# The lower query part of the prompt attention scores on all 128 rows

## The chip, the cores and the metric

The kernel runs on one core of a Trainium2 chip. The metric is device time in microseconds of one execution; before the change the median of three runs is 2746.48 us (2745.57 to 2746.51). Besides, one execution was recorded by the hardware profiler. PE is the matrix engine TensorE (PEld its weight loads, which can run under a product), DVE is VectorE, ACT is ScalarE, POOL is GpSimd, and SP issues most transfers.

## The reference

One layer of a hybrid decoder on a prompt of 1024 tokens and eight samples of eight tokens: a combined projection, then three branches (a gated linear recurrence, differential attention, cross-attention into 256 memory tokens), gates, an output projection and a feed-forward part with a convolution. All of it is float32. What the change touches is the prompt's differential attention, 8 heads with two components of 64 each:

```python
s = jnp.einsum('bqhcd,bkhcd->bhcqk', qi, k).astype(jnp.float32) * scale
s = jnp.where(kpos[None, :] <= qpos[:, None], s, NEG_INF)
p = jax.nn.softmax(s, axis=-1)
a = p[:, :, 0] - lam * p[:, :, 1]
return jnp.einsum('bhqk,bkhe->bqhe', a.astype(v.dtype), v)
```

So per head and component the scores are a product of 64-long queries and keys, for 1024 by 1024 tokens under a causal mask.

## The kernel before

Products run in a reduced float32 format (F32R). To keep precision an operand is split into an upper part (its copy in that format) and a lower part (what is left), and a product is the sum of upper times upper, upper times lower and lower times upper. The helper `mm3` (lines 162 to 165) issues those three as matmuls into one bank of PSUM; nearly all dense work goes through it.

Scores use a shorter way, since a component has only 64 features and the array has 128 rows. For component c, `qq[c]` holds the upper part of the queries in both halves of the partitions, and `kk[c]` holds the upper part of the keys in the half of its own and the lower part in the other. One product on all 128 rows (line 907) gives upper times upper and upper times lower at once. The lower part of the queries, `ql`, is one tile for both components: component 0 in partitions 0 to 63, component 1 in 64 to 127. The second product (line 909) reads only the half of its component, 64 rows of `ql` and 64 rows of `kk[c]`, and adds lower times upper into the same bank.

`attn(h)` works through the 1024 queries of a head in eight blocks of 128 (`qt`). Block `qt` needs 128 (qt + 1) keys, in chunks of at most 512 columns (at least 256 are computed), so 12 chunks per head and component, 24 pairs of products per head and 192 in all. DVE adds the mask (line 924), takes maxima (926); ACT takes exponentials (932); DVE normalizes and subtracts the second component (935 to 940). Later steps transpose the result (883) and multiply with the values.

The stage loops over eight heads. A unit projects the queries of a head (`unit(("q", h), ...)`), for three groups of tokens (384, 384 and 320 columns, 24 products each); `evac_q` takes each group out of PSUM: ACT copies the upper part of the half of its own, DVE subtracts for the lower part, POOL copies the upper part into the other half. Keys go likewise through `evac_k`. `attn(h)` is a generator in a lane of side work; `pump` advances it by rates while the next units' dense products are emitted, so that score steps lie between dense products. The tile layer places instructions on the engines' queues, derives the waits and hands out buffers; each engine then runs its queue in order.

Weights come as a stream: `Stream.ahead` loads a raw tile (`wr`, SP queue), ACT makes the upper part (`wh`, line 207) and POOL the lower (`wl`, line 209), one unit ahead, called after the first group of a unit. All these tiles, and `qq`, `ql`, `kk`, `e`, `ath`, `vh`, `pg`, share one pool of 42 buffers of 1088 columns (`slot`, `NSLOT`); eight banks of PSUM serve all products (`bank`).

Of the kernel before, what the change touches and what calls it, by code (L numbers as in the profile page):

```python
# [12 lines left out]
ALU = mybir.AluOpType  # L13
# [50 lines left out]
def layer_step(ctx: ExitStack, tc: tile.TileContext, a: dict, outs: list):  # L64
# [34 lines left out]
    def f(x):  # L99
        return x.bitcast(F32)  # L100
# [1 line left out]
    (o_yp, o_ys, o_kp, o_vp, o_mk, o_mv, o_lhp, o_lcp, o_fcp,  # L102
     o_ks, o_vs, o_lhs, o_lcs, o_fcs) = outs

# [1 line left out]
    later_q = deque()  # L106

    def later(fn, delay=1):
# [35 lines left out]
            for i in which:  # L144
                advance(lanes[i])

# [1 line left out]
    last_mm = [None]  # L148

    def load(dst, src):  # L150
        # a load is queued no earlier than the products that are being emitted
        ins = sp.dma_start(dst, src)
        if last_mm[0] is not None:
            tc.add_manual_dep(ins.ins, last_mm[0].ins.name,
                              mybir.DependencyInfo(mybir.DependencyClass.NoSync, mybir.DependencyReason.SCHED_ONLY),
                              reason="queue order")
# [7 lines left out]
        pe.matmul(ps, lhsT=lh, rhs=rl, start=False, stop=False)  # L164
        last_mm[0] = pe.matmul(ps, lhsT=ll, rhs=rh, start=False, stop=stop)  # L165

# [1 line left out]
    ident = const([128, 128], name="ident")  # L168
    pool.memset(ident, 0.0)
    pool.affine_select(out=ident, in_=ident, compare_op=ALU.not_equal, fill=1.0, base=0,  # L170
# [7 lines left out]
    pool.affine_select(out=causal, in_=causal, compare_op=ALU.is_ge, fill=NEG, base=0,  # L178
                       pattern=[[-1, 128]], channel_multiplier=1)

# [1 line left out]
    def cols(w, c0, width=128, k0=0, kn=8):  # L182
        return (w[k0 * 128:(k0 + kn) * 128, c0:c0 + width].rearrange("(k p) m -> p k m", p=128),
                [128, kn, width])
# [87 lines left out]
            for m2 in range(4):  # L272
                add(("d", g, p, m2), cols(w_down, m2 * 256, 256, g * NFG, NFG))

# [1 line left out]
    rawrow = slot([128, 6, 128], name="rawrow")  # L276
    rows = [rawrow[:, 0, :], rawrow[:, 1, :]]
    PV = {}
# [98 lines left out]
    def setup():  # L377
        put_params(1)
        ps = bank()
        pe.transpose(ps[:, 0:128], in_=frow[:, 0, :], identity=ident)  # L380
        pe.transpose(ps[:, 128:192], in_=frow[0:64, 1, :], identity=ident[:64, :64])
        act.copy(pf, ps[:, 0:192])
        ps = bank([128, NC, 32])
        for c in range(NC):
            pe.transpose(ps[:, c, :], in_=strow[:, c * 128:(c + 1) * 128], identity=ident[:32, :32])
        act.copy(stT, ps)
        yield False
        # lambda
        lprod = slot([128, 2, 64], name="lprod")
        dve.tensor_tensor(lprod[:, 0, :], lrow[:, 0, :], lrow[:, 1, :], ALU.mult)  # L390
        dve.tensor_tensor(lprod[:, 1, :], lrow[:, 2, :], lrow[:, 3, :], ALU.mult)
        dve.tensor_reduce(out=lam[:, 0:2], in_=lprod, axis=AX, op=ALU.add)
        act.activation(out=lam[:, 2:4], in_=lam[:, 0:2], func=AF.Exp)
        dve.tensor_tensor(lam[:, 4:5], lam[:, 3:4], lam[:, 2:3], ALU.subtract)
        dve.tensor_scalar(out=lam[:, 5:6], in0=lam[:, 4:5], scalar1=-LAM_INIT, scalar2=None, op0=ALU.add)
        dve.tensor_scalar(out=gsub, in0=P("g_subln"), scalar1=1.0 - LAM_INIT, scalar2=None, op0=ALU.mult)

        # softplus(-lambda), times 4 and -8
        spl = slot([128, 6, 8], name="spl")
        lo_ = PV["lru_lambda"][1]  # L400
        lm = pv[1][:, lo_:lo_ + 8]
        dve.tensor_scalar(out=spl[:, 0], in0=lm, scalar1=-1.0, scalar2=None, op0=ALU.mult)
        dve.tensor_tensor(spl[:, 1], lm, spl[:, 0], ALU.min)
        act.activation(out=spl[:, 2], in_=spl[:, 1], func=AF.Exp)
        dve.tensor_scalar(out=spl[:, 3], in0=spl[:, 2], scalar1=2.0, scalar2=None, op0=ALU.add)
        dve.reciprocal(out=spl[:, 3], in_=spl[:, 3])
        dve.tensor_tensor(spl[:, 3], spl[:, 2], spl[:, 3], ALU.mult)
        dve.tensor_tensor(spl[:, 4], spl[:, 3], spl[:, 3], ALU.mult)
        dve.memset(spl[:, 5], 1.0 / 17)
        for k in (15, 13, 11, 9, 7, 5, 3, 1):  # L410
            dve.tensor_tensor(spl[:, 5], spl[:, 5], spl[:, 4], ALU.mult)
            dve.tensor_scalar(out=spl[:, 5], in0=spl[:, 5], scalar1=1.0 / k, scalar2=None, op0=ALU.add)
        dve.scalar_tensor_tensor(out=spl[:, 5], in0=spl[:, 5], scalar=2.0, in1=spl[:, 3], op0=ALU.mult, op1=ALU.mult)
        dve.tensor_scalar(out=spl[:, 0], in0=spl[:, 0], scalar1=0.0, scalar2=None, op0=ALU.max)
        dve.tensor_tensor(spl[:, 0], spl[:, 0], spl[:, 5], ALU.add)
        for i, m in enumerate((4.0, -8.0)):
            dve.tensor_scalar(out=sp4[:, i, :], in0=spl[:, 0], scalar1=m, scalar2=None, op0=ALU.mult)
        yield False

    put_params(0)  # L420

    # memory tokens
    mss = tiny(2)
    mr = [tok_rstd(memtok[t], 128, mss[:, t:t + 1]) for t in range(2)]
    W.split(0)
# [14 lines left out]
                                 in1=mrb[:, 0:256], op0=ALU.mult, op1=ALU.mult)  # L440
        split(tf[:, 0:256], memh[c // 4][:, c % 4, :], meml[c // 4][:, c % 4, :])

    # x: three groups of tokens
    xs_d = [dpool.tile([128, T], F32, name=f"xsd{c}") for c in range(NC)]
    hh = [slot((128, T), F32R, "hh") for _ in range(NC)]
    hl = [slot((128, T), F32R, "hl") for _ in range(NC)]
# [24 lines left out]
            if c % 2 == 1:  # L471
                yield False

# [1 line left out]
    def dense(wh, wl, ah, al, g, nk=8, rate=()):  # L475
        g0, gn = GROUPS[g]
        ps = bank()
# [13 lines left out]
            pump(*[r / 2 for r in rate])  # L491

    def units(keys, evacs, ah, al, seq, rate=(1.0,), between=None):
        # several units at once, some groups of tokens for all of them before the others
        ws = [W.get(k) for k in keys]
        for n, gs in enumerate(seq):
            if n:
                between(n)
            for (wh, wl), evac in zip(ws, evacs):
                for g in gs:  # L500
                    ps = dense(lambda k: wh[:, k, :], lambda k: wl[:, k, :], ah, al, g)
                    evac(g, ps)
                    pump(*rate)
        W.ahead(1)

# [1 line left out]
    mk_d = [dpool.tile([128, 2, 256], F32, name=f"mkd{h}") for h in range(NMH)]  # L507
    mv_d = [dpool.tile([128, 2, 256], F32, name=f"mvd{h}") for h in range(NMH)]

    def mem_tail(p, kv):  # L510
        # keys of one head: feature on partitions
        ps = bank([128, 2, 256])
        for dc in range(2):
            for t in range(2):
                pe.transpose(ps[:, dc, t * 128:(t + 1) * 128], in_=kv[:, t, dc * 128:(dc + 1) * 128], identity=ident)
        kt = slot([128, 2, 256], name="mkt")
        act.copy(kt, ps)
        act.dma_start(mk_d[p], kt)
# [43 lines left out]
            e[1]()  # L562
        later_q.clear()

# [1 line left out]
    wrg = []  # L566
    for key in ("w_rg_a", "w_rg_i"):
        t = slot([128, NC, 128], name="wrg")
# [115 lines left out]
            load(pt_sb, a["page_table"].rearrange("b g -> (b g)").rearrange("(o n) -> o n", o=1))  # L684
    side.append(lru_out())

# [1 line left out]
    ms_d = [[dpool.tile([128, T], F32, name=f"msd{b}_{j}") for j in range(NC)] for b in range(2)]  # L688
    mh = [None] * NC
    ml = [None] * NC  # L690
# [60 lines left out]

    branch(0, load_lru, RB, spill_m(0), LAG0)

# [1 line left out]
    br_d = [[dpool.tile([128, T], F32, name=f"brd{b}_{h}") for h in range(NH)] for b in range(2)]  # L755
    done = [[0] * NH for _ in range(2)]
    kp_v = o_kp.rearrange("o b t h c d -> (o b t) (h c d)")
# [65 lines left out]
                pump(*RV)  # L823

    def subln_sums(sq, n):
        # sums of squares over partitions: one column of tokens per 128
        ps = bank()
        nt = (n + 127) // 128
        for i in range(nt):
# [16 lines left out]
    def attn(h):  # L846
# [5 lines left out]
        for t in range(7 + AVL + BC):  # L852
# [44 lines left out]
            if t < 8:  # L897
# [2 lines left out]
                ch = [(j, min(512, L - j)) for j in range(0, L, 512)]  # L900
                pss = {}
                for c in range(2):
                    r0 = 64 * c
                    for j, w in ch:
                        wm = max(w, 256)
                        ps = bank()
                        pe.matmul(ps[:, 0:wm], lhsT=qq[c][:, qt * 128:(qt + 1) * 128], rhs=kk[c][:, j:j + wm],
                                  start=True, stop=False)
                        last_mm[0] = pe.matmul(ps[:, 0:wm], lhsT=ql[r0:r0 + 64, qt * 128:(qt + 1) * 128],
                                               rhs=kk[c][r0:r0 + 64, j:j + wm], start=False, stop=True)  # L910
                        pss[c, j] = ps
                mx = tiny(4)
                sm = tiny(4)
# [27 lines left out]
                                         op0=ALU.mult, op1=ALU.add)  # L941
                av[qt] = e1
            yield t >= YT
# [1 line left out]
    smask = const([128, 2, 64], name="smask")  # L945
    dsel = const([128, 128], name="dsel")

# [141 lines left out]
    sample_setup()  # L1089
    for hp in range(4):  # L1090
        for h in (2 * hp, 2 * hp + 1):
            # queries: both halves of the partitions hold the upper parts; keys: upper and lower parts
            qq = [slot([128, TP], F32R, "qq") for _ in range(2)]
            ql = slot([128, TP], F32R, "ql")
            HALF = (slice(0, 64), slice(64, 128))

            def evac_q(g, ps):
# [3 lines left out]
                for c in range(2):  # L1101
                    own, other = HALF[c], HALF[1 - c]
                    act.copy(qq[c][own, cs], ps[own, 0:n])
                    dve.tensor_tensor(ql[own, cs], ps[own, 0:n], f(qq[c][own, cs]), ALU.subtract)
                    pool.tensor_copy(qq[c][other, cs], qq[c][own, cs])
                if g == 2:
                    act.copy(QKS[:, 0, h, :], ps[:, n:n + TS])

# [39 lines left out]
            lanes[1].append(sattn(h))  # L1148


# [1 line left out]
    MQ = {}  # L1152
    MSQ = {}
    for i in range(2):
# [185 lines left out]

    branch(2, load_br(1), RH, final_m)

# [1 line left out]
    x2_d = [dpool.tile([128, T], F32, name=f"x2d{c}") for c in range(NC)]  # L1344
    ob = [slot(name="ob") for _ in range(NC)]
    ssq = {}
# [23 lines left out]
    HOLD = 6  # L1370

    def residual(src, g):
        # tiles of the residual stream, read two ahead
        g0, gn = GROUPS[g]
        ts_ = {}

# [66 lines left out]
    drain((0,))  # L1443
    side.append(post_mix(2))

# [1 line left out]
    sfc = a["state_ffn_conv"].rearrange("o b j d -> (o b j) d")  # L1447
    fcs_v = o_fcs.rearrange("o b j d -> (o b j) d")
    acc = [None] * NC
# [56 lines left out]
        yield False  # L1506

    def ffn_tail_cut(j, pads):
        # as ffn_tail, one group of tokens after the other
        g, i = divmod(j, NFG)  # L1510
        fo = FO[g]
        cs = [slot(name="cv") for _ in range(2)]
# [54 lines left out]
            sp.dma_start(dst, yo[i][0:n])  # L1567
        yield False

    # the norm's factor is one number per token once the tokens are on the partitions  # L1570
    xtl, ytl, sct, ptl = {}, {}, {}, {}

    def pieces(g):
# [155 lines left out]
```

## Time and profile before

| | before |
|---|---|
| median of three runs | 2746.48 us |
| profiled execution, span from first to last instruction | 2744.3 us |
| PE busy | 2674.3 us (97%) |
| weight loads busy | 2536.1 us (92%) |
| DVE, ACT, POOL busy | 1254.8, 992.1, 891.0 us |
| mean granted TensorE clock | 0.987 of full speed |
| prompt attention, 500 to 1120 us: PE, DVE | 611.58, 389.68 us of 620 |

No time of the profiled execution beside its span is given; the median of the runs lies 2.2 us above that span. Busy time is the sum of an engine's instructions where they overlap counted once. Matmuls are pipelined: the shown duration of a product is longer than the distance to the next one, so what a product takes of the engine is read from the starts of successive products. A weight load that runs under the product before it costs nothing visible; one that starts only where its own product starts stands in the way.

### The profile page before, as it was taken

The page shows a single profiled execution, that of the slowest core. Times are in us where ns is not written, and L with a number is a line of the kernel's source. Part 1 is how long each engine was busy: PE and PEld are TensorE (multiplying, and loading weights), DVE is VectorE, ACT ScalarE, POOL GpSimd, SP SyncE. Part 2 cuts the span into 40 slices and gives each one's busy share as a digit, 9 for nine tenths or more (in the row PEclk, how much of TensorE's full clock was granted, in tenths as well). Part 3 has the DMA queues.
Part 4 walks back from the last instruction along what each step waited for, and adds up shares of the span by engine and source line. Part 5 has one row for each costly group of instructions (what it writes and reads, how often), then busy time and mean ns, then how long its engine had stood idle before and what let it go on. Part 6 is the DMA issues. An engine that isn't in the chain of part 4 may idle for free. (4 is left out here: it accounts for less than half of the span.)

```text
span 2744.3 us, 42962 instructions
## 1 busy us (share of the span) xinstructions
PE 2674.3 (97%) x16884; PEld 2536.1 (92%) x16884; DVE 1254.8 (46%) x2442; ACT 992.1 (36%) x2071; POOL 891.0 (32%) x891
## 2 busy tenths in 40 slices
PE   8999999999999999999999999989999999999997
PEld 7999899987888888899979999989999999999996
DVE  6465510267676665633234213277143343434357
ACT  6566521245445454434430212343321222222232
POOL 4355422423232333221111121353333333334234
PEclk9999999999999999999999999989999999999998
DMA  8311022221221212234755434132212111111133
GB/s 300 114 39 39 24 72 74 69 63 52 65 66 60 64 57 79 69 111 133 228 193 185 152 95 142 51 106 79 56 32 64 31 41 54 41 47 48 39 109 115
DMA packets 293472, 237.32 MB, mean 86 GB/s; under 512 B 16912, under 2 KB 276793, under 8 KB 293269
## 3 DMA queue, kind: packets, MB, share of 16 engines
q1 hardware_dynamic: 286484, 225.91, 26.3%
q10 hardware_dynamic: 6784, 8.65, 0.9%
q8 instruction: 133, 2.18, 0.3%
q14 instruction: 71, 0.57, 0.1%
HBM read 182.11 MB, written 52.40 MB: 85 GB/s over the span
## 5 line engine op out<-in xcount | busy, mean ns | idle before, releaser
L209 POOL TENSOR_TENSOR wl<-wr,wh 128x1024 fp32r<-128x1024 f32 x192 | 472.5, 2465 | 746.1 <-ACT wh L207 499.7
L163 PE MATMUL ps<-hh,wh 128*128 128x384 f32 (+1 forms) x1536 | 515.9, 336 | 3.3 <-DVE y L1015 1.2
L165 PE MATMUL ps<-hh,wl 128*128 128x384 f32 (+1 forms) x1536 | 504.9, 329 | 4.2 <-POOL wl L209 4.2
L164 PE MATMUL ps<-hl,wh 128*128 128x384 f32 (+1 forms) x1536 | 504.7, 329 | 0.0
L163 PE MATMUL ps<-h2h,wh 128*128 128x384 f32 (+1 forms) x1152 | 376.8, 328 | 3.2 <-ACT h2h L159 3.2
L164 PE MATMUL ps<-h2l,wh 128*128 128x384 f32 (+1 forms) x1152 | 377.2, 327 | 1.0 <-DVE h2l L160 1.0
L165 PE MATMUL ps<-h2h,wl 128*128 128x384 f32 (+1 forms) x1152 | 376.8, 327 | 0.9 <-POOL wl L209 0.9
L163 PEld LDWEIGHTS ps<-hh,wh 128*128 128x128 f32 x1536 | 290.5, 189 | 18.2 <-issue 11.1
L207 ACT CAST wh<-wr 128x1024 fp32r<-128x1024 f32 x199 | 208.0, 1051 | 255.6 <-PE ps L164 74.5
L165 PEld LDWEIGHTS ps<-hh,wl 128*128 128x128 f32 x1536 | 290.2, 189 | 7.1 <-POOL wl L209 4.8
L164 PEld LDWEIGHTS ps<-hl,wh 128*128 128x128 f32 x1536 | 290.6, 189 | 1.2 <-issue 1.0
L163 PE MATMUL ps<-bh,wh 128*128 128x384 f32 (+1 forms) x768 | 251.3, 328 | 0.0
L164 PE MATMUL ps<-bl,wh 128*128 128x384 f32 (+1 forms) x768 | 251.0, 327 | 0.0
L165 PE MATMUL ps<-bh,wl 128*128 128x384 f32 (+1 forms) x768 | 249.8, 327 | 0.0
L163 PEld LDWEIGHTS ps<-h2h,wh 128*128 128x128 f32 x1152 | 217.1, 189 | 3.7 <-ACT h2h L159 3.6
L164 PEld LDWEIGHTS ps<-h2l,wh 128*128 128x128 f32 x1152 | 217.2, 189 | 1.6 <-DVE h2l L160 1.5
L165 PEld LDWEIGHTS ps<-h2h,wl 128*128 128x128 f32 x1152 | 217.0, 188 | 1.1 <-POOL wl L209 1.1
L598 DVE TENSOR_SCALAR cv<-up,pf 128x1024 f32<-128x1024 f32 (+2 forms) x52 | 58.4, 1125 | 346.3 <-ACT up L586 176.1
L586 ACT COPY up<-ps 128x384 f32<-128x384 f32 (+1 forms) x144 | 63.9, 445 | 366.0 <-PE ps L165 350.5
L165 PE MATMUL ps<-ffh,wl 128*128 128x384 f32 (+1 forms) x576 | 189.3, 333 | 1.2 <-POOL wl L209 1.2
L164 PE MATMUL ps<-ffl,wh 128*128 128x384 f32 (+1 forms) x576 | 190.3, 332 | 0.0
L163 PE MATMUL ps<-ffh,wh 128*128 128x384 f32 (+1 forms) x576 | 188.1, 335 | 2.2 <-DVE acc L1679 1.6
(345 smaller groups left out, 5115.6 us busy)
## 6 DMA issues: line engine op xcount, KB each, us to landing
wr<-in_w_in_dram SPq DMA_DIRECT2D x72, 512.0 KB
wr<-in_w_up_dram SPq DMA_DIRECT2D x48, 512.0 KB
wr<-in_w_down_dram SPq DMA_DIRECT2D x32, 512.0 KB
msd<-sig SPq DMA_DIRECT2D x16, 544.0 KB
brl<-brd SPq DMA_DIRECT2D x16, 544.0 KB
mi<-msd SPq DMA_DIRECT2D x16, 544.0 KB
wr<-in_w_mem_kv_dram SPq DMA_DIRECT2D x16, 512.0 KB
pg<-in_cache_k_dram SPq DMA_DIRECT2D x128, 64.0 KB
```

The lines of the kernel that those rows point to most:

```text
L163: pe.matmul(ps, lhsT=lh, rhs=rh, start=start, stop=False)
L164: pe.matmul(ps, lhsT=lh, rhs=rl, start=False, stop=False)
L165: last_mm[0] = pe.matmul(ps, lhsT=ll, rhs=rh, start=False, stop=stop)
L207: (dve.tensor_copy if i == 1 else act.copy)(hi, t)
L209: eng.tensor_tensor(lo, t, f(hi), ALU.subtract)
L586: act.copy(pad[:, hist + g0:hist + g0 + n], ps[:, 0:n])
L598: dve.tensor_scalar(out=o, in0=i, scalar1=wcol(0), scalar2=bcol, op0=ALU.mult, op1=ALU.add)
```

## The change

`ql` becomes two tiles, one for each component. As `qq[c]`, `ql[c]` holds the lower part of its component's queries in both halves: DVE writes the half of its own as before, and a new POOL copy fills the other. The second product reads all 128 rows of `ql[c]` and `kk[c]`; it thereby also adds lower times lower, which was left out before. The first product and all that follows are unchanged. (The diff also removes comments, not shown.)

```diff
@@ attn(h), score step
                 for c in range(2):
-                    r0 = 64 * c
                     for j, w in ch:
                         wm = max(w, 256)
                         ps = bank()
                         pe.matmul(ps[:, 0:wm], lhsT=qq[c][:, qt * 128:(qt + 1) * 128], rhs=kk[c][:, j:j + wm],
                                   start=True, stop=False)
-                        last_mm[0] = pe.matmul(ps[:, 0:wm], lhsT=ql[r0:r0 + 64, qt * 128:(qt + 1) * 128],
-                                               rhs=kk[c][r0:r0 + 64, j:j + wm], start=False, stop=True)
+                        last_mm[0] = pe.matmul(ps[:, 0:wm], lhsT=ql[c][:, qt * 128:(qt + 1) * 128],
+                                               rhs=kk[c][:, j:j + wm], start=False, stop=True)
@@ per head
             qq = [slot([128, TP], F32R, "qq") for _ in range(2)]
-            ql = slot([128, TP], F32R, "ql")
+            ql = [slot([128, TP], F32R, "ql") for _ in range(2)]
@@ evac_q
                     act.copy(qq[c][own, cs], ps[own, 0:n])
-                    dve.tensor_tensor(ql[own, cs], ps[own, 0:n], f(qq[c][own, cs]), ALU.subtract)
+                    dve.tensor_tensor(ql[c][own, cs], ps[own, 0:n], f(qq[c][own, cs]), ALU.subtract)
                     pool.tensor_copy(qq[c][other, cs], qq[c][own, cs])
+                    pool.tensor_copy(ql[c][other, cs], ql[c][own, cs])
```

## Rows read from the trace of the kernel before

**Rows 1.** Part 1 of the page: busy time of each engine, share of the span, instructions.

```profile
PE 2674.3 (97%) x16884; PEld 2536.1 (92%) x16884; DVE 1254.8 (46%) x2442; ACT 992.1 (36%) x2071; POOL 891.0 (32%) x891
```

**Rows 2.** Busy time by stretch: the stage of prompt attention.

```profile
500.00:1120.00 620.00, 611.58 (x3903) 518.23 (x3902) 389.68 (x1123) 285.80 (x847) 201.06 (x325) 0.99 0.21 62
```

**Rows 3.** Line 909 alone: durations in ns min/median/max, then its shapes.

```profile
L909 PEld LDWEIGHTS ps<-kk,ql x192: 182/183/286, 528.6 to 1114.7; 64*128 64x128 f32 x192
L909 PE MATMUL ps<-kk,ql x192: 379/466/793, 528.6 to 1114.8; 64*128 64x512 f32 x96, 64*128 64x256 f32 x64, 64*128 64x384 f32 x32
```

**Rows 4.** Timeline of PE, five steps apart: start, duration, line, operation, shape.

```profile
877.81 0.40 PE L907 MATMUL ps<-kk,qq 128*128 128x512 f32 x1
...
878.56 0.50 PE L907 MATMUL ps<-kk,qq 128*128 128x512 f32 x1
878.99 0.50 PE L909 MATMUL ps<-kk,ql 64*128 64x512 f32 x1
879.42 0.50 PE L907 MATMUL ps<-kk,qq 128*128 128x512 f32 x1
...
880.27 0.44 PE L165 MATMUL ps<-hh,wl 128*128 128x384 f32 x1
880.55 0.34 PE L163 MATMUL ps<-hh,wh 128*128 128x384 f32 x1
```

**Rows 5.** Timeline of the weight loads in the same stretch; idle time before in brackets.

```profile
877.64 0.19 PEld L907 LDWEIGHTS ps<-kk,qq 128*128 128x128 f32 x1
878.13 0.18 PEld L909 LDWEIGHTS ps<-kk,ql 64*128 64x128 f32 x1 [0.31 <-issue]
878.55 0.19 PEld L907 LDWEIGHTS ps<-kk,qq 128*128 128x128 f32 x1 [0.24 <-issue]
```

**Rows 6.** Timeline of PE: a score pair of 256 columns.

```profile
528.88 0.39 PE L907 MATMUL ps<-kk,qq 128*128 128x256 f32 x1
529.20 0.38 PE L909 MATMUL ps<-kk,ql 64*128 64x256 f32 x1
529.50 0.39 PE L801 MATMUL ps<-wh,hh 128*128 128x256 f32 x1
```

**Rows 7.** Timeline of PE: a score pair of 384 columns.

```profile
625.88 0.44 PE L907 MATMUL ps<-kk,qq 128*128 128x384 f32 x1
626.25 0.43 PE L909 MATMUL ps<-kk,ql 64*128 64x384 f32 x1
626.61 0.33 PE L1056 MATMUL ps<-ident,t 128*128 128x128 f32 x1
```

**Rows 8.** Timeline of PE: first and last of 12 dense products of 384 columns.

```profile
873.22 0.34 PE L163 MATMUL ps<-hh,wh 128*128 128x384 f32 x1
...
875.13 0.34 PE L165 MATMUL ps<-hh,wl 128*128 128x384 f32 x1
```

**Rows 9.** Timeline of PE: first and last of 10 value products of 256 columns.

```profile
882.95 0.28 PE L165 MATMUL ps<-ath,vl 128*128 128x256 f32 x1
...
884.02 0.28 PE L165 MATMUL ps<-ath,vl 128*128 128x256 f32 x1
```

**Rows 10.** Waits of PE in the stage: us in total, times, longest.

```profile
PE ps L907 <- ACT e L932: 2.2, 4, 1.3
```

**Rows 11.** Waits of DVE in the stage.

```profile
DVE ps L924 <- PE ps L909: 39.9, 45, 7.2
DVE y L926 <- PE ps L909: 20.1, 22, 2.8
```

**Rows 12.** Groups in the stage: busy us, mean ns, idle before and its releasers.

```profile
L1105 POOL CAST qq<-qq 64x384 fp32r<-64x384 f32 (+1 forms) x48 | 26.4, 551 | 135.4 <-ACT qq L1103 92.9 <-DVE y L936 33.5 <-issue 6.2
```

**Rows 13.** Timeline of POOL: the latest split of a key weight tile.

```profile
1041.95 2.39 POOL L209 TENSOR_TENSOR wl<-wr,wh 128x1024 fp32r<-128x1024 f32 x1
```

**Rows 14.** Timeline of PE: the first product that reads that split.

```profile
1048.60 0.35 PE L165 MATMUL ps<-hh,wl 128*128 128x384 f32 x1
```

**Rows 15.** Waits of the load queue in the stage.

```profile
SPq L152 <- DVE e L940: 60.4, 5, 19.3
```

## The prediction, made before the changed kernel was run

> **What bounds the kernel now.** I read part 1 of the page first: TensorE (PE) is busy for 97% of the span, and no other engine passes 46% [rows 1]. The reader is to see that time is taken from this kernel only by taking time from PE. The change touches one stage, so the second view is the table by stretch: between 500 and 1120 us PE is busy for 611.6 of 620 us, DVE for 389.7, ACT for 285.8, POOL for 201.1 [rows 2]. The weight loads, which elsewhere nearly keep step with PE, fall behind here: 518.2 us. Third, the line of the second score product alone: 192 products and 192 loads, of 512 (96), 256 (64) and 384 columns (32), on 64 rows; a product is shown with a median of 466 ns [rows 3]. Fourth, the two timelines of PE, matmuls and weight loads, which show why that is long.
>
> In the timeline of a score step the products of 512 columns start every 0.43 us: 878.56, 878.99, 879.42 [rows 4]. Ordinary products run back to back: 12 of 384 columns take 11 steps in 1.91 us, 0.174 us each [rows 8], and 10 of 256 columns 9 steps in 1.07 us, 0.119 us each [rows 9]. The slope between them is 0.055 us for 128 columns, so I estimate 0.228 us for 512 columns. The score products take nearly twice that. The loads say where it goes. The load of line 907 behind an ordinary product starts at 877.64, 0.17 us ahead of its own product at 877.81: it runs under the product before. The load of line 909 (64 rows) starts only at 878.13, after 0.31 us without a load, and the next load of 907 (128 rows) at 878.55, again after 0.24 us, with its product 0.01 us behind [rows 4, 5]. So wherever the row count of the loaded weights changes, 128 to 64 or back, the load waits for the product before it, and loading and streaming no longer overlap. A load alone takes 0.18 to 0.19 us.
>
> **The change part by part.**
>
> *The second product on 128 rows.* The number of products, their columns and their order in the program stay. What goes is the change of row count at both ends of each of the 192 second products. By size, a pair now against a pair at ordinary spacing:
> - 512 columns: 0.43 + 0.43 = 0.86 us [rows 4] against 2 x 0.228 = 0.456; 96 x 0.404 = 38.8 us.
> - 384 columns: 626.61 - 625.88 = 0.73 us [rows 7] against 2 x 0.174 = 0.348; 32 x 0.382 = 12.2 us.
> - 256 columns: 529.50 - 528.88 = 0.62 us [rows 6] against 2 x 0.119 = 0.238; 64 x 0.382 = 24.4 us.
>
> Together 75.4 us, or 384 boundaries of about 0.196 us. A pair that stands between ordinary products shows a shorter first step (0.32 instead of 0.43), but its successor pays the difference: line 165 at 880.27 is followed after 0.28 us instead of 0.174 [rows 4]. Counted by boundaries the two kinds are worth the same. The one price not in the trace is the 512-column step on 128 rows behind another of 128 rows. Its bounds are 0.228 (the slope) and 0.238 (twice the 256-column step); the upper one takes 1.9 us from the gain. I take the slope.
>
> Weighed against this: the Trainium skill, TensorE: Matmul & The Clock Gate, under The mechanism (Part 3), says that a weight load overlaps running products only when its row group differs. By that sentence a load on all 128 rows could never run under a product on all 128 rows, and the change would be worth nothing. The trace speaks against it: the load at 877.64 ran under the 128-row product that started at the same moment [rows 5].
>
> *The POOL copies.* 48 more copies of 64 partitions, priced as the 48 copies of the upper part: 0.551 us mean, 26.4 us of POOL [rows 12]. POOL goes from 201 to 227 us in a stage of about 550: under half. They are not free of a path: in a group of tokens, POOL holds two more copies and waits for DVE's subtraction before it reaches its next job, which behind group 0 is the split of the next unit's weights. The latest such split of a key unit runs 1041.95 to 1044.34 [rows 13]; its first reader starts at 1048.60 [rows 14]. That is 4.3 us of cover, against two copies (1.1 us) and a wait that I bound by 0 and 2 us, the length of a few DVE instructions. The cover holds, so I cost it at nothing; without cover it would be 8 units x 3 us = 24 us. Below nothing it cannot be, since only work is added.
>
> *The DVE subtraction* only writes to another tile: no change.
>
> *The second tile.* One more of the 42 buffers for each live head. From the code, 16 hold the normalized input for the whole stage, one the sample queries; each live head then keeps 6 instead of 5, and weights, values, exponentials, transposed weights of attention and pages share the rest. That some transfers already wait for a buffer shows in the load queue: 60.4 us in five waits for the last reader of an exponential [rows 15]. PE does not wait for weights in this stage; its largest wait group is 2.2 us, for the read of score banks, and the eight groups of that view sum to 8.0 us [rows 10]. So a buffer more costs something between nothing and what a late load costs (rival below). I take nothing of its own.
>
> *What is late next.* PE runs about 75 us ahead of where it was, and the softmax chain has to follow. DVE now idles 39.9 + 20.1 = 60.0 us until a second product has ended [rows 11]. That slack can shrink without anyone else noticing; the remaining 15 us of the 75 would have to be PE waiting. Bounds for the giveback: 0 and 15 us. DVE at 389.7 us in some 545 is 72% busy, so bursts will now and then hold score banks; I take the middle, 8 us, a doubling of the 8.0 us of waits.
>
> **Sum.** 2744.3 - 75.4 + 8 = 2676.9 us of span. The median of the runs is 2746.48, 2.2 us above the profiled span, so 2679 us.
>
> **Rivals.**
>
> *The softmax chain takes half back.* Mechanism: scores hold up to four of eight banks in a step, and DVE and ACT empty them. If DVE's slack is in the wrong places, PE waits at each of the 64 steps for 0.6 us: 38 us, time 2709. For it: DVE is the second busiest engine of the stage. Against it: PE barely waits for it now [rows 10], and dense products of other units lie between the steps to fill in.
>
> *Nothing goes.* If the load of line 909 waits not for the change of row count but for another reason (a load on all rows that must wait for any product on all rows, or two products into one bank with one moving tile), the waits stay: 2746. The sentence of the skill named above is the first of these. Against it: dense products follow each other on all rows and into one bank at 0.174 us [rows 8].
>
> *Slower: the buffers run out.* Place: the load queue. The queue is in order, so one load that waits for a buffer holds the weights behind it. Some 24 weight units are split in the stage, with at least 4.3 us of cover [rows 13, 14]. At 8 us of added lateness for each, PE would wait 24 x 3.7 = 89 us, more than the 75 saved: 2760. It decides from about 7.4 us of lateness on every unit (4.3 + 75/24). The five waits of up to 19.3 us speak for it [rows 15]; that no wait of PE for weights is seen today speaks against.
>
> **How the numbers follow.** Forecast 0.78; half given back 0.14; nothing 0.04; slower 0.04. The likeliest case alone spans 2669 (no giveback, and a few us less of other waits or reduced clock) to 2692 (15 us of giveback, 1.9 us for the wide step, a few us of copies). The range reaches towards the half case: 2667 to 2704. About 0.2% (5.5 us) is what a measurement can tell here. Faster 0.94, taking the forecast, the half case and part of the third; same 0.02; slower 0.04.
>
> **What would show it.** In the changed trace: line 909 with 128 rows; score products of 512 columns 0.23 us apart, and their loads starting under the product before, without the 0.24 us idle entries; the row of the stage 65 to 75 us shorter with PE still above 97%; weight loads' busy time in it unchanged near 518 us; DVE's waits for line 909 well under 60 us; POOL about 26 us busier. Everything after the stage should be the same, only earlier. Wrong would be: loads of line 909 still late although the rows match (then the cause is not the row count), or the spacing as forecast but PE waiting for ACT, DVE or a weight split by more than 20 us (then the term for what is late next was too small).

## The result, and the profile after

The changed kernel takes 2704.69 us (median of four runs, 2703.62 to 2709.35), against 2746.49 us in the same session: a ratio of 0.985, interval 0.9836 to 0.9864. It is 41.8 us faster; 67.5 were forecast, and the time lies 0.7 us above the range. The profiled execution has a span of 2702.4 us.

Part 1 of the page after answers to [rows 1]:

```profile
PE 2611.6 (97%) x16884; PEld 2529.7 (94%) x16884; DVE 1247.4 (46%) x2442; ACT 990.8 (37%) x2071; POOL 914.5 (34%) x939
```

The products and loads are as many as before, PE's share is as high, and POOL has gained 48 instructions and 23.6 us. The table by stretch, the stage first and then the rest, answers to [rows 2]; a row holds the stretch, its length, the busy time of PE, PEld, DVE, ACT and POOL with their instructions, the granted clock as a share of full speed, and share and GB/s of the transfers:

```profile
500.00:1077.60 577.60, 550.58 (x3902) 512.68 (x3901) 381.45 (x1116) 282.42 (x840) 223.94 (x373) 0.99 0.22 67
1077.60:2702.40 1624.80, 1584.52 (x10017) 1546.58 (x10015) 640.56 (x1048) 478.43 (x890) 493.55 (x411) 0.99 0.30 93
```

The rest lasts 1624.8 us; before it was 2744.3 - 1120 = 1624.3. So all of the change lies in the stage: 620.0 to 577.6 us, 42.4 us less where 65 to 75 were forecast, and PE is busy for 95% of it, not for over 97%. Busy time of the weight loads stayed near 518 (512.7), that of DVE near 390 (381.5). Now the second product's own line, as [rows 3]:

```profile
L908 PEld LDWEIGHTS ps<-kk,ql x192: 187/189/338, 525.3 to 1074.6; 128*128 128x128 f32 x192
L908 PE MATMUL ps<-kk,ql x192: 274/366/628, 525.4 to 1074.8; 128*128 128x512 f32 x96, 128*128 128x256 f32 x64, 128*128 128x384 f32 x32
```

It has 128 rows, and its median duration went from 466 to 366 ns. The timelines of PE and of the weight loads in a score step of 512 columns answer to [rows 4, 5]:

```profile
858.22 0.40 PE L906 MATMUL ps<-kk,qq 128*128 128x512 f32 x1
858.46 0.40 PE L908 MATMUL ps<-kk,ql 128*128 128x512 f32 x1
858.70 0.40 PE L906 MATMUL ps<-kk,qq 128*128 128x512 f32 x1
858.93 0.39 PE L908 MATMUL ps<-kk,ql 128*128 128x512 f32 x1
859.15 0.39 PE L906 MATMUL ps<-kk,qq 128*128 128x512 f32 x1
```

```profile
858.23 0.19 PEld L908 LDWEIGHTS ps<-kk,ql 128*128 128x128 f32 x1
858.46 0.19 PEld L906 LDWEIGHTS ps<-kk,qq 128*128 128x128 f32 x1
858.70 0.19 PEld L908 LDWEIGHTS ps<-kk,ql 128*128 128x128 f32 x1
858.93 0.19 PEld L906 LDWEIGHTS ps<-kk,qq 128*128 128x128 f32 x1
```

The products start 0.23 to 0.24 us apart instead of 0.43, and each load starts with the product before it, 0.23 us ahead of its own; no idle time stands before a load. This part of the forecast came out as written. But the waits of PE in the stage, as [rows 10], have changed:

```profile
PE ps L906 <- ACT e L931: 7.2, 5, 2.6
PE ps L1055 <- DVE t L1050: 3.9, 1, 3.9
PE ps L883 <- ACT e L931: 3.5, 1, 3.5
```

Eight groups with 8.0 us in all have become 22 groups with 26.6 us, more than the 20 us that the prediction named as a sign that its term for what is late next was too small. The largest is again the wait of a first product for ACT's exponentials, which empty its bank: 7.2 instead of 2.2 us. DVE's waits for second products, as [rows 11], shrank:

```profile
DVE ps L923 <- PE ps L908: 17.0, 15, 7.3
...
DVE y L925 <- PE ps L908: 7.2, 10, 2.7
```

They went from 60.0 to 24.2 us, 36 us less, not the 60 that the prediction let vanish for nothing. The copies take as much of POOL as was worked out (26.8 us, forecast 26.4), and POOL waits 15.3 us for DVE in front of them:

```profile
L1106 POOL CAST ql<-ql 64x384 fp32r<-64x384 f32 (+1 forms) x48 | 26.8, 560 | 17.1 <-DVE ql L1104 15.3 <-DVE y L929 0.9
```

### The profile page after: what moved, and what is told of

It reads as the page before. It is cut to its first block, busy times and chain, and to the rows that moved or that the text cites. A ratio compares the mean times of both kernels' runs of the same rounds, so it can differ in the third digit from the quotient of the medians.

```text
span 2702.4 us, 43028 instructions
## 1 busy us (share of the span) xinstructions
PE 2611.6 (97%) x16884; PEld 2529.7 (94%) x16884; DVE 1247.4 (46%) x2442; ACT 990.8 (37%) x2071; POOL 914.5 (34%) x939
## 5 line engine op out<-in xcount | busy, mean ns | idle before, releaser
L207 ACT CAST wh<-wr 128x1024 fp32r<-128x1024 f32 x199 | 207.9, 1050 | 252.7 <-PE ps L164 74.6
```

The costliest lines, as they stand in the source:

```text
L207: (dve.tensor_copy if i == 1 else act.copy)(hi, t)
```

## The experiments

Theory A: the price of 33.6 us (75.4 worked out, 41.8 measured) comes from what the change adds, the tile and the copies. Theory B: it comes from PE being faster, because the softmax chain does not empty the score banks in time. Each run is timed beside the kernel before on the same chip; times are medians, and ratios are to the kernel before.

**The rows alone.**

```diff
-lhsT=ql[r0:r0 + 64, qt * 128:(qt + 1) * 128], rhs=kk[c][r0:r0 + 64, j:j + wm]
+lhsT=ql[:, qt * 128:(qt + 1) * 128], rhs=kk[c][:, j:j + wm]
```

> The kernel before with one edit: the second product reads all 128 rows of the one ql tile and of kk[c] (so its sum also takes products of the other component's lower queries). No second tile, no POOL copy, and every engine's instruction order is that of the kernel before. Theory A (the added tile and copies, with the order of work that they bring, took back about 25 us of the 75): 2746 - 75 + 8 = 2679, within 2673 to 2687. Theory B (the softmax chain cannot empty the score banks as fast as TensorE now fills them, whoever adds what): 2700 to 2706, as the changed kernel.

2693.89 us (2693.22 to 2696.1), ratio 0.9804 (0.9788 to 0.982): 53.0 us faster than before, between the two expectations, and faster than the changed kernel. In the two traces all 16884 products, 2442 DVE, 2071 ACT and 891 POOL instructions stand in the same order, by line and columns, as before the change.

So nothing differs but the rows of 192 products, and 22.4 of the 75.4 us are missing without a tile or a copy. The remaining 10.8 us up to the changed kernel come with what it adds. Here the second product also adds the other component's lower queries times the lower keys, which is not wanted but a product of two lower parts, as small as the one that the kernel before left out; for its speed the kernel needs neither second tile nor copies. Table by stretch, the largest wait group, and the timeline of PE around one such wait, all of the rows-only run:

```profile
500.00:1067.50 567.50, 548.27 (x3904) 510.67 (x3904) 383.48 (x1122) 284.29 (x842) 201.01 (x325) 0.99 0.23 68
1067.50:2692.20 1624.70, 1584.88 (x10017) 1546.08 (x10015) 640.76 (x1043) 478.34 (x890) 493.10 (x411) 0.99 0.30 93
```

```profile
PE ps L907 <- ACT e L932: 8.2, 9, 2.1
```

```profile
778.58 0.39 PE L909 MATMUL ps<-kk,ql 128*128 128x512 f32 x1
778.80 0.39 PE L907 MATMUL ps<-kk,qq 128*128 128x512 f32 x1
779.03 0.40 PE L909 MATMUL ps<-kk,ql 128*128 128x512 f32 x1
781.56 0.50 PE L907 MATMUL ps<-kk,qq 128*128 128x512 f32 x1 [2.13 <-ACT e L932]
```

The stage shrank by 52.5 us. The waits in it sum to 18.9 us in that view, 10.9 more than before; the group above went from 2.2 to 8.2 us. In the timeline the products run at 0.22 to 0.23 us, and then the third chunk of the step waits for a bank until 781.56: a gap of 2.53 us. A bank that comes late also holds back the load of the product that is to fill it, without PE being shown as idle. Loads of the step at 566.76, which stood behind such a wait:

```profile
567.33 0.19 PEld L907 LDWEIGHTS ps<-kk,qq 128*128 128x128 f32 x1 [0.27 <-ACT e L932]
568.00 0.19 PEld L907 LDWEIGHTS ps<-kk,qq 128*128 128x128 f32 x1 [0.37 <-ACT e L932]
```

Both start with their own product instead of with the one before, and the products of that step start up to 0.34 us apart instead of 0.23.

**The chain made shorter.**

```diff
-dve.reduce_max(out=mx[:, 2 * i + c:2 * i + c + 1], in_=pss[c, j][:, 0:w], axis=AX)
+dve.reduce_max(out=mx[:, 2 * i + c:2 * i + c + 1], in_=pss[c, j][:, 0:128], axis=AX)
```

> The run with rows only (2693.9), but DVE takes each maximum over the first 128 columns of a score bank instead of all of it (a softmax comes out the same from any shift that does not overflow). DVE's 192 maxima fall from 549 ns to about 280 ns, 50 us in the stage, and each bank is free sooner; the order of work is almost that of the rows-only run. Theory B (the 22 us that the rows-only run lost of the 75 are waits for score banks behind DVE and ACT): 10 to 18 us less, 2676 to 2684. Theory C (they come from the order in which work was queued, not from the speed of the softmax chain): within 4 us of 2694.

2677.19 us (2675.67 to 2678.5), ratio 0.9743 (0.9726 to 0.976): 16.7 us less than with the rows alone, as theory B expects. DVE's group of maxima and the stage in this run:

```profile
L926 DVE TENSOR_REDUCE y<-ps 128x1 f32<-128x128 f32 x192 | 50.9, 282 | 17.3 <-PE ps L909 16.8
```

```profile
500.00:1051.00 551.00, 540.02 (x3908) 509.69 (x3907) 339.76 (x1121) 284.34 (x844) 200.44 (x325) 1.00 0.24 70
```

The maxima take 50.9 us instead of 101.2, and the stage ends after 551.0 us: 69 of the 75 us are there. PE gets faster although no instruction of PE was touched: its waits in the stage fall from 18.9 to 10.7 us, and the 6.8 us that the rows-only run's stage has at the lower of TensorE's two clock levels (granted clock 0.50 of full speed) are gone. So PE had been waiting for the softmax chain, which DVE's maxima lead.

Two things limit this. The order is not quite the same: at least 410 of the 16884 products stand at another place in PE's queue than in the rows-only run. And the narrow maximum on the kernel before was not run, so how much it is worth without faster products is not shown; PE was idle there for only 8.4 us of the stage [rows 2].

**Copies and tile apart.** Three kernels on 128 rows, on top of the rows-only run:

```diff
# copies only
+spare = ...
+m = min(n, 368)
+pool.tensor_copy(spare[other, 0:m], ql[own, g0:g0 + m])
# tile only: two tiles by groups of tokens
-dve.tensor_tensor(ql[own, cs], ps[own, 0:n], f(qq[c][own, cs]), ALU.subtract)
+dve.tensor_tensor(ql[g // 2][own, cs], ps[own, 0:n], f(qq[c][own, cs]), ALU.subtract)
-lhsT=ql[:, qt * 128:(qt + 1) * 128]
+lhsT=ql[qt // 6][:, qt * 128:(qt + 1) * 128]
# copies free: as copies only, but
+pool.tensor_copy(spare[other, 0:m], qq[c][own, g0:g0 + m])
```

> The run with rows only, plus 48 POOL copies of the lower query part into a spare tile that nothing reads (368 of 384 columns), outside the 42 buffers: the copies without the second tile. If the copies are what separates the changed kernel (2704.7) from the rows-only run (2693.9): 2702 to 2707. If the buffer is: 2692 to 2697.

2703.36 us, 0.9837 (0.982 to 0.9854): 9.5 us more than the rows alone.

> The run with rows only, but the lower query part lies in two tiles, one for the first two groups of tokens and one for the third: one more buffer for each live head, no copy and no instruction more. If the buffer is what separates the changed kernel from the rows-only run: 2702 to 2707. If the copies are: 2692 to 2697. If both only matter through the order of work that they bring, anything within 10 us of 2694.

2694.11 us, 0.9806 (0.979 to 0.9823): nothing. The buffer is free here.

> The copies-only run (2703.4), but the spare copies read the upper part, which is there by then, so POOL never waits for DVE's subtraction; the order of work is nearly the same. If POOL's waiting for DVE (15 us in 18 waits in the changed kernel) is the price of the copies: 2693 to 2698. If their place and time in the queue, or the order of work: 2701 to 2705.

2703.05 us (2698.63 to 2705.36), 0.9846 (0.983 to 0.9862): POOL's wait for DVE is not the price.

So it is the copies, with the order that they bring. Where one place of their price lies is seen in the changed kernel's POOL queue, then DVE's, then PE's:

```profile
614.05 0.19 POOL L1047 TENSOR_SCALAR y<-y 128x1 f32<-128x1 f32 x1 [0.25 <-ACT t L1046]
614.52 0.50 POOL L1105 CAST qq<-qq 64x384 fp32r<-64x384 f32 x1 [0.28 <-ACT qq L1103]
615.04 0.51 POOL L1106 CAST ql<-ql 64x384 fp32r<-64x384 f32 x1
615.64 2.40 POOL L209 TENSOR_TENSOR wl<-wr,wh 128x1024 fp32r<-128x1024 f32 x1
617.99 0.56 POOL L1048 TENSOR_TENSOR y<-y,mhalf 128x1 f32<-128x1 f32 x1
```

```profile
618.60 0.30 DVE L923 TENSOR_TENSOR ps<-ps,causal 128x128 f32<-128x128 f32 x1
...
621.52 0.56 DVE L1104 TENSOR_TENSOR ql<-ps,qq 64x384 fp32r<-64x384 f32 x1
...
622.36 0.35 DVE L1050 TENSOR_SCALAR t<-ps,y 128x128 f32<-128x128 f32 x1
```

```profile
618.57 0.34 PE L908 MATMUL ps<-kk,ql 128*128 128x384 f32 x1
622.86 0.45 PE L1055 MATMUL ps<-ident,t 128*128 128x128 f32 x1 [3.95 <-DVE t L1050]
```

POOL's step of the sample branch (the power, line 1048) now stands behind the weight split and ends at 618.55. The DVE step that reads it, line 1050, stands behind a score step in DVE's queue and runs at 622.36. PE, which has that branch's transpose next, waits 3.95 us. In the rows-only run the power runs ahead of the split:

```profile
613.45 0.50 POOL L1105 CAST qq<-qq 64x384 fp32r<-64x384 f32 x1 [0.28 <-ACT qq L1103]
614.04 0.56 POOL L1049 TENSOR_TENSOR y<-y,mhalf 128x1 f32<-128x1 f32 x1
614.56 2.41 POOL L209 TENSOR_TENSOR wl<-wr,wh 128x1024 fp32r<-128x1024 f32 x1
```

There PE has no such wait. The run with copies alone has it too:

```profile
PE ps L1057 <- DVE t L1052: 4.3, 2, 3.9
```

**Copies made cheaper or later, in the changed kernel.**

```diff
# zeros, once a head, instead of the copies
+for c in range(2):
+    pool.memset(f(ql[c][HALF[1 - c], :]), 0.0)
# copies late: only after the third group
+if g == 2:
+    for c in range(2):
+        pool.tensor_copy(ql[c][HALF[1 - c], :], ql[c][HALF[c], :])
# both
-pool.tensor_copy(ql[c][other, cs], ql[c][own, cs])
```

> The changed kernel, but the other half of each ql tile is filled with zeros when the tile is made (two POOL memsets a head in place of six copies, and no wait of POOL for DVE); the lower times lower part is left out as before the change. If theory A is about the POOL copies: 2679 to 2690. If it is about buffers: 2702 to 2706. Theory B: 2702 to 2706.

2693.52 us (2691.16 to 2697.26), 0.9805 (0.9789 to 0.9822): between the expectations, and as the rows alone, with the second tile.

> The changed kernel with two copies of the lower part a head (all 1024 columns, after the third group of tokens) in place of six, so that POOL has no such copy in front of the weight split behind group 0. If the 10 us that the copies cost come from standing in POOL's queue ahead of the weight split and of the sample branch's small steps: 2692 to 2697. If from POOL's time as such (18 us of copies remain): 2700 to 2706.

2698.86 us (2697.3 to 2700.31), 0.9827 (0.9811 to 0.9844): 5.8 us less than the changed kernel, between the expectations. The 3.9 us wait for the sample branch is gone. Some 5 us above the rows alone stay, but the table by stretch of this run puts most of them elsewhere:

```profile
500.00:1069.30 569.30, 548.45 (x3907) 510.68 (x3907) 376.89 (x1116) 282.72 (x840) 215.11 (x341) 0.99 0.23 68
1069.30:2697.30 1628.00, 1589.70 (x10018) 1551.15 (x10016) 643.89 (x1048) 477.98 (x890) 492.97 (x411) 0.98 0.30 93
```

The stage is 1.8 us longer than with the rows alone (567.5), and the rest, in which the edit changes nothing, 3.3 us (1628.0 against 1624.7). So in this execution the copies made late cost the stage hardly anything.

**Both prices together.** The changed kernel with the narrow maximum:

> The changed kernel with each maximum over 128 columns, as in the narrow-max run. Theory B says that what PE loses in this stage is waiting behind the softmax chain: about 17 us less than the changed kernel, 2684 to 2692; the 10 us of the copies stay if they come by POOL (then near 2688), and go too if they also come by way of score banks (2676 to 2682).

2688.75 us (2688.43 to 2695.87), 0.9799 (0.9781 to 0.9817): 15.9 us less than the changed kernel, and 11.6 more than the rows alone with the narrow maximum. The two prices add up, as expected if the copies do not work by way of score banks.

**Tile and copies on 64 rows.** The changed kernel with `ql[c][64 * c:64 * c + 64, ...]` and the same half of `kk[c]`, with and without the copies:

> The changed kernel with its second tile and its POOL copies, but the second product on the 64 rows of its component, as before. Theory A: the added work costs something here too, up to 25 us, so 2755 to 2772. Theory B: added tile and copies are hidden, 2744 to 2750.

2762.89 us, 1.0056 (1.0039 to 1.0073): 16.0 us slower than before.

> Two ql tiles of which only the half of the own component is written and read: no POOL copies, second product on 64 rows. It shows the price of the buffer alone. If buffers are what theory A is about: as the run with copies and 64 rows, 2755 to 2772. If it is the POOL copies: 2744 to 2750. Theory B: 2744 to 2750.

2757.42 us (2752.53 to 2759.96), 1.0032 (1.0021 to 1.0043): 10.6 us slower, with no instruction added. The tile that costs nothing on 128 rows costs 10.6 here, so it is not the buffer as such. The stage of this run, and the longest of five stretches in it with the clock at its lower level:

```profile
500.00:1130.40 630.40, 619.67 (x3899) 524.52 (x3899) 386.43 (x1122) 284.85 (x843) 200.90 (x325) 0.98 0.21 61
965.60:975.80 10.20, 10.20 (x37) 6.48 (x37) 6.30 (x19) 4.12 (x14) 1.33 (x6) 0.50 0.00 1
```

The five take 27.2 us, against 6.8 in the stage before; in the one shown, dense products of 256 columns stand 0.21 us apart instead of 0.119 [rows 9]. The 20.4 us more are worth some 9 us, an estimate from these two spacings, and PE's idle time in the stage is 2.3 us longer (10.7 against 8.4). Together that is the price. With the copies it is the same 27.2 us at the lower level, and idle time of 14.4 us. So it is mostly the clock; each of the five stretches begins behind a wait of PE of 0.4 to 2.1 us, but why the clock fell more often here, through the order that another set of tiles brings or otherwise, stays open.

**Order alone.** The rows-only run with `RA = (1.6, 0.9)` instead of `(1.7, 0.9)`:

> The run with rows only, with the rate at which score steps are emitted between the dense products of query and key units lowered from 1.7 to 1.6: the same work in another order, a measure of how much order alone moves the time. If order alone is worth 10 us: away from 2694 by 5 us or more, either way. If not: 2690 to 2698.

2708.18 us (2707.29 to 2711.93), 0.9858 (0.984 to 0.9877): 14.3 us slower with the same work, and PE stands idle in the stage for 28.6 us instead of 19.2. Some 2300 products stand at another place in PE's queue, far more than the 194 of the run with copies only. Differences of 10 us between kernels whose orders differ are therefore no proof of the edit's own cost.

**The boundary by another way.**

```diff
+# all first products of the step, then
+for c in range(2):
+    r0 = 64 * c
+    for j, w in ch:
+        last_mm[0] = pe.matmul(pss[c, j][:, 0:wm], lhsT=ql[r0:r0 + 64, ...], rhs=kk[c][r0:r0 + 64, ...], ...)
```

> The kernel before, 64-row second products kept, but in each of the 64 score steps all first products come before all second ones: the row count changes twice a step, 128 times, instead of 384. If the price hangs on the change of row count (0.196 us each): 256 x 0.196 = 50 us less before waits, and with 10 to 22 us of waits as in the rows-only run 2706 to 2720; loads of neighbouring 64-row products run under each other. If every 64-row load is late whatever stands before it: 128 x 0.196 = 25 us less before waits, 2722 to 2735.

2730.11 us (2727.28 to 2730.87), 0.9939 (0.9923 to 0.9956): 16.5 us faster, less than either. The grouping was not kept: the tile layer put many pairs together again. Two pieces of its timeline, a grouped step and one that was not:

```profile
528.55 0.48 PE L906 MATMUL ps<-kk,qq 128*128 128x256 f32 x2
528.96 0.38 PE L913 MATMUL ps<-kk,ql 64*128 64x256 f32 x2
529.27 0.39 PE L801 MATMUL ps<-wh,hh 128*128 128x256 f32 x1
```

```profile
786.11 0.50 PE L913 MATMUL ps<-kk,ql 64*128 64x512 f32 x1
786.54 0.38 PE L906 MATMUL ps<-kk,qq 128*128 128x256 f32 x1
786.86 0.38 PE L913 MATMUL ps<-kk,ql 64*128 64x256 f32 x1
787.17 0.49 PE L906 MATMUL ps<-kk,qq 128*128 128x512 f32 x1
```

Counted over the trace, 283 changes of row count at score products are left; the same count gives 379 in the kernel before. 96 x 0.196 = 18.8 us, close to the measured 16.5. But the run does not isolate the price of a change: in 37 places two second products on opposite halves, as in the first piece, ran at the same time, which saves a product each, some 6 us by the ordinary spacings. It agrees with a price that goes with the number of changes; the number that was to be expected was wrong.

## Why the prediction was wrong

*The second product on 128 rows: right in its mechanism, some 6 us too large.* Spacing, hidden loads and the missing idle entries came as worked out; the 512-column step is 0.23 to 0.24 us, between or near its bounds of 0.228 and 0.238. The Trainium skill, TensorEngine Tiling (Array Packing), Key Properties, says that a change of tiling mode, not of the tile, drains TensorE; the trace agrees, with 0.18 to 0.2 us for each change. The Trainium skill's sentence on row groups, weighed in the prediction, does not hold here: every load of the step above runs under a product on the same 128 rows. The size is read best from the narrow-max run, in which PE waits little and the clock does not fall in the stage. Its stage is 69.0 us shorter than before. Adding the 2.6 us by which PE's idle time is longer there (11.0 against 8.4), and taking off some 3 us for the 6.8 us at the lower clock that the kernel before had, the row changes are worth some 69 us, an estimate, where the prediction had 75.4. The wide step is 1 to 2 us of the difference; the rest of it was not taken apart.

*What is late next: mis-sized, the step that failed.* Its term was 8 us with bounds of 0 and 15. With nothing added (rows alone) 22.4 us are missing; some 6 of them belong to the term above, so this one measures some 16 us: 10.9 us more of waits, and some 5 us behind waits, in products whose own load was held back as shown at 567.33. The fault was to treat DVE's 60.0 us of waiting as slack that can go first. A wait in one step cannot be spent in another: PE stands still at particular steps, 2.53 us at 779 us for example, while DVE in the changed kernel still waits 24.2 us in others. The narrow maximum shows that the chain is the cause of most of it: 16.7 us came back when only DVE was relieved, some 3 of them by way of the clock, and 15.9 in the changed kernel.

*The POOL copies: costed at nothing, the second step that failed; measured 9.5* (copies alone). The cover of 4.3 us was of the right kind but for the wrong reader: the weight split was not late. Late was the sample branch, whose small POOL step came to stand behind the split. Against the rows alone, the stage of the changed kernel is 10.1 us longer: PE's idle time is 7.8 us longer, half of it that wait of 3.9 us, and the clock is at its lower level for 13.6 us instead of 6.8, worth some 3 us. The wait is gone in the run with late copies, and with it 5.8 us of the kernel's time. How much of the rest is POOL's time and how much the changed order stays open; order alone is worth 14.3 us in one run. Taking that small step off POOL was not run.

*The DVE subtraction and the second tile: right.* The tile costs nothing on 128 rows (2694.11 against 2693.89).

*The rivals.* Half given back named the right mechanism and 2709, 4.3 us from the result; it had 0.14. That its time is so near is luck: it put 38 us on the chain, which took some 16. Nothing goes and the slower case are refuted by the rows alone and by the tile alone. The result lies 25.7 us above the forecast: some 6 us from the first term, some 8 from the second and some 10 from the copies. All three point the same way, so the range, which ended at 2704, did not hold them.

## What to carry to other kernels

Where neighbouring products load weights of different row counts, look at the starts of the loads: if one starts only when the product before has been streamed, make the counts equal, and first ask whether data that already lies in the other rows will do, before copies are paid for. When PE is sped up inside a stage, do not subtract another engine's total waiting from what it will cost; look at which step the next engine is late in. An edit that adds instructions also reorders queues, and here order alone moved the time by as much as the edit's side costs. And before a difference of 10 us is put down to an edit, add up how long the clock stood at its lower level in either run.

## What the runs showed of the hardware

Two 64-row products on opposite halves of the rows ran together: in the grouped run's first piece, two of 256 columns, started 0.004 us apart, and the next product came 0.31 us after them, which before was the time of one [rows 6]. The run has 37 such pairs, 0.003 to 0.007 us apart.

The granted clock fell to 0.50 in three stretches of the changed kernel's stage, each within or right behind a gap on PE (4.3, 3.7 and 2.8 us between the starts of two products, from 618.6, 648.2 and 789.5 us on):

```profile
621.60:628.40 6.80, 5.54 (x21) 4.98 (x22) 2.55 (x9) 1.76 (x6) 0.79 (x3) 0.50 0.01 2
652.30:655.70 3.40, 3.20 (x7) 2.32 (x8) 1.95 (x8) 3.04 (x12) 2.17 (x6) 0.50 0.00 0
792.20:795.60 3.40, 3.35 (x11) 2.74 (x12) 3.34 (x7) 2.92 (x10) 0.00 (x0) 0.51 0.02 5
```

13.6 us in all at the lower level of 1.2 GHz, where the kernel before had 6.8 us in its stage. So these waits cost more than their own length: products of 512 columns stand 0.43 us apart in these stretches instead of 0.23.
